# Strassen products for the FFN input of a two-layer diffusion trunk, and a new place for layer 1's tables

## The chip, the cores and the metric

The kernel runs on one core of a Trainium2 chip. The time is device microseconds (us) of one execution. Five engines take part: TensorE (PE, matmuls; PEld is its weight load), VectorE (DVE), ScalarE (ACT), GpSimd (POOL), and SyncE (SP), which issues most of the DMAs. Each engine runs its own instructions in order, and semaphores tie the engines together.

## The reference, cut to what matters

The program computes one step of a trunk of two layers over 640 tokens (512 latent, 128 context) of width 1024. Each layer mixes the tokens by four branches (a state-space model, a Fourier transform, attention, a short convolution), merges them by gates, projects, and then runs an FFN:

```
x  = x + g_m * mix
xn = rms_norm(x, lp['norm_ffn_g']) * (1 + sc_f) + sh_f
x  = x + g_f * swiglu(xn, lp['w_ffn_in'], lp['w_ffn_out'])
```

Here `swiglu` is `(silu(xn @ Wg) * (xn @ Wu)) @ Wo`, `Wg` and `Wu` being the halves of `w_ffn_in`. The FFN width is 2816, that is 22 tiles of 128 channels. Shift, scale and gate (`sh_f`, `sc_f`, `g_f` and the same for the mixer) are six sections of a modulation, `silu(cond) @ w_ada + b_ada`, for each layer and stream. Everything is float32.

## The kernel before, in words

**Layout.** All activations are channel-major: a tile holds 128 channels by 640 tokens, in two halves of 320 (`HALF`), each half in a PSUM bank of its own. A float32 product is made of three: an operand `x` is split into a rounded `xh` and a rest `xl`, a weight into `whi` and `wlo`, and the sum is `whi*xh + wlo*xh + whi*xl`. So one chunk (128 output channels, 1024 input channels) is 8 k-tiles x 3 terms x 2 halves = 48 matmuls of 128x128 by 320 columns, all issued at line 238 (`mm`). In the trace `main` is the PSUM tile of a chunk (two banks, two such tiles), `side` that of the smaller products.

**Weights** (`weights`, L317 on). A chunk's weights are loaded by SP to `wraw`, ACT casts them to `whi` (L319), DVE subtracts to get `wlo` (L320). There are three tiles each of `wraw`, `whi`, `wlo` (`WBUFS`). Around a norm, four chunks are subtracted by POOL instead of DVE (`SPARE`, L332 and L333).

**Order.** PE's order is written by hand: a main stream of products, and side chains (generators) whose steps are put between them at `tick()` when an estimated clock says that they are ready. On the other engines a scheduler orders the work, where the weights run up to 400 instructions ahead (`AHEAD`). [...]

**Stages of a layer.** `mixer_in` (input projection; latents, attention, convolution), `mixer_out` (state-space blocks, gates, merges), `tail` (output projection, norm, FFN). In the first layer the state-space tables of that layer (`ssm_tables`) are made beside `mixer_in`, the modulations' sections 2 to 5 beside `mixer_out`. The tables and rotations of layer 1 and all six modulation sections of layer 1 are made beside `tail` of layer 0. A modulation step on DVE is `ada_j` at L572.

**The FFN** (`tail`, L1488 on). `normed` makes the eight operand tiles `xs[k] = (xh, xl)` from the norm: a DVE multiplication to a scratch tile `hh` or `hl` (L458), an ACT bias and rounding to `xh` (L461), and a DVE operation for `xl` (L463). The first pair of chunks runs beside it. Then, for f = 0 to 21, `ffn_in(f)` makes a gate chunk and an up chunk, ACT takes the silu (L1521), DVE multiplies (`f_s`, L1523), and the product is split to `hh` and `hl`. `FFN_ROUNDS` are (0,8), (8,16), (16,22): after a round's tiles are there, eight output chunks of `wfo` run over them and are added to `x` (L1332, `residual`). One tile of the next round is made ahead of the output chunks. In the last round the last three output chunks go by halves of the tokens, and then the next layer's norm, or the output, follows.

The core of the FFN's input before:

```
def ffn_in(f):
    pg = self.chunk(A["wfi"][l, f], KD, xs) if f else first[0]
    s = self.t(p, [128, NT], "f_s", bufs=2)
    nc.scalar.activation(out=two(s), in_=pg[:, :, :HALF], func=AF.Silu)
    pu = self.chunk(A["wfi"][l, NF + f], KD, xs) if f else first[1]
    self.anchor = nc.vector.tensor_mul(out=two(s), in0=pu[:, :, :HALF], in1=two(s))
    self.split(hi, lo, s)
    hs[f] = (hi, lo)
```

## Time and profile before

| | us |
|---|---|
| median of 3 runs (2669.23 to 2675.43) | 2671.71 |
| span of the profiled execution | 2683.6 |
| PE busy | 2618.7 (98%), 18518 instructions |
| DVE busy | 1534.2 (57%) |
| ACT busy | 883.2 (33%) |
| POOL busy | 187.9 (7%) |

The profiled execution is 11.9 us (0.45%) longer than the median of the timed runs. The busy shares are means over stages that differ; the windows in the section of rows give them stage by stage. Their bounds are read off the instructions: a layer's first latent copy and its last attention DMA bound the first window (59.5 to 422.5, and 1401.1 to 1755.2), from there to the first residual is the second (to 832.0 and to 2148.6), and the first to the last `f_s` product of the FFN is the third (910.1 to 1331.8 and 2229.6 to 2637.9). PEclk in a row is the granted clock as a share of the full 2.4 GHz.

### The profile page before, as it was taken

To read this page: it belongs to the slowest core of one execution; us is meant where nothing else is said; L and a number is where in the kernel's file an instruction comes from. 1 tells how busy PE (TensorE), PEld (TensorE's weight loads), DVE (VectorE), ACT (ScalarE), POOL (GpSimd) and SP (SyncE) were. 2 spreads that over 40 slices of the span, in tenths; PEclk is the share of its full clock that TensorE was granted. 3 is DMA by queue.
4 is the path that set the end of the run, shared out by engine and by line. 5 is a ranking of instruction groups with operands and counts; after the bars stand their busy time and mean duration, and the time that the engine had idled before them with its cause. 6 is when DMAs were issued, how large, how long until landed. Compare 5 with 4: busy or idle time off the path is not lost.

```text
span 2683.6 us, 44723 instructions
## 1 busy us (share of the span) xinstructions
PE 2618.7 (98%) x18518; PEld 2505.7 (93%) x18518; DVE 1534.2 (57%) x3061; ACT 883.2 (33%) x1393; POOL 187.9 (7%) x316
## 2 busy tenths in 40 slices
PE   7999999999999999999999899999999999999999
PEld 5987898999999899999979779999999999999999
DVE  5888764776557579989453356654454444232323
ACT  5334544233224422221243244433323233212211
POOL 0110000111001100000020000011100010000000
PEclk8999999999999999999999999999999999999999
DMA  6442115574435255655232221155532322222222
GB/s 250 135 150 85 56 61 173 176 216 140 126 121 172 63 165 181 202 179 166 80 119 75 60 63 52 50 155 160 149 99 80 107 74 71 79 72 79 71 75 75
DMA packets 118747, 312.78 MB, mean 117 GB/s; under 512 B 35344, under 2 KB 46160, under 8 KB 118288
## 3 DMA queue, kind: packets, MB, share of 16 engines
q1 hardware_dynamic: 99376, 250.52, 30.7%
q0 software_dynamic: 16432, 55.39, 6.1%
q10 hardware_dynamic: 2736, 4.01, 0.4%
q8 instruction: 146, 2.39, 0.4%
q14 instruction: 57, 0.47, 0.1%
HBM read 267.07 MB, written 42.80 MB: 115 GB/s over the span
## 4 chain that ended last, share of the span: by engine, by line
PE 84%; issue 9%; DVE 2%; ACT 2%; DMA 2%; POOL 0%; ACTq 0%; SPq 0%; DVEq 0%; POOLq 0%
PE main L238 74%; PE side L238 9%; PE side L242 1%; DMA s_EF<-d_et 1%; DVE xl L463 1%; DVE wlo L320 0%; ACT whi L319 0%; ACT pq L897 0%; DVE hl L458 0%; ACT P L794 0%; DMA yb<-d_br 0%; POOL d_r L1136 0%; DVE hh L458 0%; DVE sm L791 0%; ACT xh L461 0%
## 5 line engine op out<-in xcount | busy, mean ns | idle before, releaser
L238 PE MATMUL main<-xh,whi 128*128 128x320 f32 x3488 | 831.2, 315 | 1.7 <-ACT xh L461 1.3
L238 PE MATMUL main<-xl,whi 128*128 128x320 f32 x3488 | 815.8, 311 | 1.7 <-DVE xl L463 1.5
L238 PE MATMUL main<-xh,wlo 128*128 128x320 f32 x3488 | 813.5, 310 | 0.0
L319 ACT CAST whi<-wraw 128x1024 fp32r<-128x1024 f32 (+1 forms) x302 | 312.3, 1034 | 1162.4 <-PE main L238 675.9
L238 PEld LDWEIGHTS main<-xh,whi 128*128 128x128 f32 x3488 | 585.7, 189 | 25.1 <-issue 19.9
L238 PEld LDWEIGHTS main<-xl,whi 128*128 128x128 f32 x3488 | 590.4, 189 | 6.7 <-DVE xl L463 6.4
L320 DVE TENSOR_TENSOR wlo<-wraw,whi 128x1024 fp32r<-128x1024 f32 (+1 forms) x302 | 367.7, 1218 | 397.0 <-ACT whi L319 395.7
L238 PEld LDWEIGHTS main<-xh,wlo 128*128 128x128 f32 x3488 | 590.5, 189 | 0.0
L238 PE MATMUL main<-yb,whi 128*128 128x320 f32 x1152 | 231.3, 312 | 2.1 <-ACT yb L319 2.1
L572 DVE SCALAR_TENSOR_TENSOR ada_j<-ada,ada_c 128x1024 bf16<-128x1024 f32 x160 | 195.1, 1219 | 3.8 <-DMA ada<-wada 2.9
L238 PEld LDWEIGHTS main<-yb,whi 128*128 128x128 f32 x1152 | 184.7, 189 | 3.0 <-ACT yb L319 2.4
L1332 DVE SCALAR_TENSOR_TENSOR x<-main,ada,x 128x320 f32<-128x320 f32 (+2 forms) x192 | 75.6, 434 | 177.2 <-PE main L238 176.9
L238 PE MATMUL main<-hh,whi 128*128 128x320 f32 x704 | 167.4, 311 | 0.0
L238 PE MATMUL main<-hh,wlo 128*128 128x320 f32 x704 | 166.2, 309 | 0.0
L238 PE MATMUL main<-hl,whi 128*128 128x320 f32 x704 | 166.2, 309 | 0.0
L238 PE MATMUL main<-yb,wlo 128*128 128x320 f32 x576 | 131.9, 310 | 0.0
L1523 DVE TENSOR_TENSOR f_s<-main,f_s 128x640 f32<-128x640 f32 x44 | 36.2, 824 | 150.6 <-PE main L238 150.6
L238 PEld LDWEIGHTS main<-hh,whi 128*128 128x128 f32 x704 | 119.0, 188 | 3.5 <-issue 3.5
L238 PEld LDWEIGHTS main<-hh,wlo 128*128 128x128 f32 x704 | 119.2, 188 | 0.0
L238 PEld LDWEIGHTS main<-hl,whi 128*128 128x128 f32 x704 | 119.2, 188 | 0.0
L238 PEld LDWEIGHTS main<-yb,wlo 128*128 128x128 f32 x576 | 97.1, 189 | 0.0
L794 ACT ACTIVATE P<-side,sm,rq 128x640 f32<-128x640 f32 (+1 forms) x80 | 63.9, 800 | 98.7 <-DVE sm L792 97.0
(320 smaller groups left out, 2761.3 us busy)
## 6 DMA issues: line engine op xcount, KB each, us to landing
ada<-wada SPq DMA_DIRECT2D x96, 512.0 KB, 4.4
wraw<-wfi SPq DMA_DIRECT2D x88, 512.0 KB, 3.6
wraw<-wgate SPq DMA_DIRECT2D x64, 512.0 KB, 3.6
wraw<-win SPq DMA_DIRECT2D x50, 512.0 KB, 3.7
wraw<-wbr SPq DMA_DIRECT2D x32, 512.0 KB, 3.7
wraw<-wfo SPq DMA_DIRECT2D x32, 512.0 KB, 3.6
d_f<-t_G POOLq DMA_DIRECT2D x16, 512.0 KB, 4.1
d_et<-t_et POOLq DMA_DIRECT2D x16, 512.0 KB, 5.1
```

Of the source, the lines that this page charges most:

```text
L238: self.nc.tensor.matmul(out, lhsT, rhs, **kw)
L242: self.nc.tensor.transpose(out, in_, ident)
L319: self.nc.scalar.copy(out=hi, in_=src)
L320: self.nc.vector.tensor_sub(out=lo, in0=src, in1=hi.bitcast(F32))
L463: nc.vector.scalar_tensor_tensor(out=xl[:, a:b], in0=t[:, a:b], scalar=B[:, s:s + 1], in1=xh.bitcast(F32)[:, a:b], op0=ALU.add, op1=ALU.su ...
L572: nc.vector.scalar_tensor_tensor(out=junk, in0=w, scalar=1.0, in1=sc[:, s, :], op0=ALU.mult, op1=ALU.mult, accum_out=self.ada[l][:, o + t, ...
L794: nc.scalar.activation(out=p[:, :nk].rearrange("p (a b) -> p a b", a=s.shape[1]), in_=s, func=AF.Exp, scale=rq, bias=small[:, 1:2], accum_ ...
L1332: self.anchor = nc.vector.scalar_tensor_tensor(out=x[:, o:o + n], in0=p, scalar=gcol[:, s:s + 1], in1=x[:, o:o + n], op0=ALU.mult, op1=ALU ...
L1523: self.anchor = nc.vector.tensor_mul(out=two(s), in0=pu[:, :, :HALF], in1=two(s))
```

## The change

Five things are altered; comments are taken out of the file too, so its line numbers differ.

1. **Seven half products.** For f = 2 to 21 (`PLAIN = 2`) the pair of a gate and an up chunk is seen as a 2x2 block product, the blocks being the two halves of the input channels (4 k-tiles each) by the two halves of the tokens on one side, and the gate and up weights by the same halves on the other. Seven products of 4 k-tiles and 320 columns take the place of eight. `strassen_weights` adds four sums of weight halves (128x512 each) to the two loaded chunks, `sums` makes the four sums of operand tiles (T1 to T4) after f = 0, and `place` writes T1 over the second half of `xs[0..3]`.
2. **PSUM.** In `tail` the main tiles are four of one bank each (`main_bank`), where there were two of two banks.
3. **Rounds.** `FFN_ROUNDS` is (0,6), (6,12), (12,18), (18,22), and `hh` and `hl` have 7 tiles in place of 9, to make room.
4. **Tables.** Layer 1's `ssm_tables` and `rotations` move from `tail` of layer 0 to `mixer_in` of layer 1, where layer 0's stand too.
5. **Modulations.** Beside `tail` of layer 0 stand sections 0 and 1 of layer 1 alone; sections 2 to 5 move to `mixer_out` of layer 1.

```
-FFN_ROUNDS = [(0, 8), (8, 16), (16, 22)]
+FFN_ROUNDS = [(0, 6), (6, 12), (12, 18), (18, 22)]
+PLAIN = 2
-TABLES_PACE = (1.5, 3.0)
+TABLES_PACE = 1.5
-MOD_PACE = (10.5, 7.0)
+MOD_PACE = (10.5, 12.0)
...
+    def strassen_weights(self, first, second, ahead=AHEAD):
...
+            a, b = raw
+            pair([a[:, :n]])
+            sa, sb = [self.t(self.sp, [128, 1024], "wsum", bufs=2) for _ in range(2)]
+            V.tensor_add(out=sa[:, :m], in0=b[:, :m], in1=b[:, m:n])
+            V.tensor_add(out=sa[:, m:n], in0=sa[:, :m], in1=a[:, :m])
+            pair([sa[:, :n]])
+            V.tensor_add(out=sb[:, :m], in0=sa[:, m:n], in1=a[:, m:n])
+            pair([sb[:, :m], b[:, m:n]])
+            V.tensor_add(out=sb[:, m:n], in0=a[:, :m], in1=b[:, :m])
+            pair([sb[:, m:n]])
+        return out
+
+    def strassen(self, first, second, forms, use):
+        ws = self.strassen_weights(first, second)
+        a, b, c, d = [self.main_bank()[:, :HALF] for _ in range(4)]
+        self.bank = (self.bank + 1) % 4
+        n = first.shape[1] // 2
+        for i, (bank, x, step, start) in enumerate((
+                (a, "B11", "P1", True), (b, "B21", "P2", True), (c, "T1", "P5", True), (a, "T2", "U2", False),
+                (c, "B22", "P3", False), (d, "T4", "P4", True), (a, "T3", "U3", False))):
+            hi, lo, o = ws[i]
+            for k in range(n):
+                xh, xl = forms[x][k]
+                for t, (ww, xx) in enumerate(((hi, xh), (lo, xh), (hi, xl))):
+                    self.mm(bank, ww[:, o + 128 * k:o + 128 * k + 128], xx, start=start and k == 0 and t == 0,
+                            stop=k == n - 1 and t == 2, skip_group_check=not start)
+                self.tick()
+            use(step, bank)
...
+    def sums(self, pool, tags, bs, B, xs):
...
+        for k in range(KD):
+            for a, b, s in ((0, LAT, 0), (LAT, NT, 1)):
+                nc.scalar.activation(out=bs[k][:, a:b], in_=bs[k][:, a:b], func=AF.Identity, bias=B[:, k, s:s + 1])
...
+            V.tensor_sub(out=t1, in0=b11, in1=b12)
+            V.scalar_tensor_tensor(out=t24[:, :HALF], in0=t1, scalar=-1.0, in1=b22, op0=ALU.mult, op1=ALU.subtract)
+            V.tensor_sub(out=t3[:, o], in0=b22, in1=b12)
+            V.tensor_add(out=t24[:, HALF:], in0=t24[:, :HALF], in1=b21)
+            todo = [(t24, ("T2", "T4"))] + ([(t3, ("T3", "T3"))] if k % 2 else [])
+            for t, names in todo:
+                hi, lo = [self.t(pool, [128, NT], tag, F32R, bufs=6) for tag in ("th", "tl")]
+                self.split(hi, lo, t)
...
+        def place():
+            for k in range(n):
+                hi, lo = forms["T1"][k]
+                self.split(hi, lo, t1s[k // 2][:, k % 2 * HALF:k % 2 * HALF + HALF])
...
+            def halves(f):
...
+                def use(step, ps):
+                    if step in ("P1", "U2", "P5"):
+                        nc.scalar.copy(out={"P1": s0, "U2": s1, "P5": u1}[step], in_=ps)
+                    elif step == "P4":
+                        nc.scalar.activation(out=u0, in_=ps, func=AF.Copy, scale=-1.0)
+                    elif step == "U3":
+                        self.anchor = V.tensor_tensor(out=two(u), in0=ps.unsqueeze(1).to_broadcast([128, 2, HALF]),
+                                                      in1=two(u), op=ALU.add)
+                    else:
+                        o = s0 if step == "P2" else s1
+                        V.tensor_add(out=o, in0=ps, in1=o)
+                        nc.scalar.activation(out=o, in_=o, func=AF.Silu)
+                self.strassen(A["wfi"][l, f], A["wfi"][l, NF + f], forms, use)
+                V.scalar_tensor_tensor(out=s, in0=u, scalar=-1.0, in1=s, op0=ALU.mult, op1=ALU.mult)
+                split_h(f, s)
...
-                hi = self.t(p, [128, NT], "hh", F32R, bufs=9)
-                lo = self.t(p, [128, NT], "hl", F32R, bufs=9)
+                hi = self.t(p, [128, NT], "hh", F32R, bufs=7)
+                lo = self.t(p, [128, NT], "hl", F32R, bufs=7)
...
-                self.tables = self.side(self.layer_tables(pt, l + 1, TABLES_PACE[1]))
-                self.modulations(pt, l + 1, range(6), MOD_START[1], MOD_PACE[1], 2)
+                self.modulations(pt, l + 1, range(2), MOD_START[1], MOD_PACE[1], 1)
...
-            if l == 0:
-                self.modulations(p, 0, range(2, 6), MOD_START[0], MOD_PACE[0], 1)
+            self.modulations(p, l, range(2, 6), MOD_START[0], MOD_PACE[0], 1)
```

In all, PE's order has 480 matmuls fewer than before, DVE's 521 instructions more and ACT's 401 more.

On DVE, inside the FFN of layer 1 away from its ends, one pair of chunks before is two weight subtractions, the product `f_s` and its rest `hl`:

```order
L320 TENSOR_TENSOR wlo_23972<-wraw_23969,whi_23971 128x1024 [waits DMAHW4_49,Activation_49]
L1523 TENSOR_TENSOR f_s_23850<-main_23858,f_s_23850 128x640 [waits PE_49,Activation_49]
L320 TENSOR_TENSOR wlo_24032<-wraw_24029,whi_24031 128x1024 [waits DMAHW5_49,Activation_49]
L320 TENSOR_TENSOR hl_23909<-f_s_23850,hh_23908 128x640 [waits Activation_49]
L320 TENSOR_TENSOR wlo_24089<-wraw_24086,whi_24088 128x1024 [waits DMAHW6_49,Activation_49]
```

The same pair now, from the addition of P2 (L1656) on; L1652 is the addition of U3, L1659 the last product, `wsum` the weights' sums, and the four groups of `wlo` are called A1 (22907), A2 (22915), A3 (22920, in two) and A4 (22927):

```order
L1656 TENSOR_TENSOR f_s_22768<-main_3283_22799,f_s_22768 128x320 [waits PE_49]
L321 TENSOR_TENSOR wlo_22907<-wraw_22902,whi_22906 128x1024 [waits Activation_49]
L1656 TENSOR_TENSOR f_s_22768<-main_3284_22800,f_s_22768 128x320 [waits PE_49,Activation_49]
L321 TENSOR_TENSOR wlo_22915<-wsum_22910,whi_22914 128x1024 [waits Activation_49]
L1652 TENSOR_TENSOR f_u_22769<-main_3282_22798,f_u_22769 128x640 [waits PE_49,Activation_49]
L321 TENSOR_TENSOR wlo_22920<-wsum_22911,whi_22919 128x512 [waits DVE_49,Activation_49]
L321 TENSOR_TENSOR wlo_22920<-wraw_22903,whi_22919 128x512 [waits Activation_49]
L389 TENSOR_TENSOR wsum_23042<-wraw_23035 128x512 [waits DMAHW3_49,DVE_49]
L1659 SCALAR_TENSOR_TENSOR f_s_22768<-f_u_22769,f_s_22768 128x640 [waits DVE_49]
L390 TENSOR_TENSOR wsum_23042<-wsum_23042,wraw_23034 128x512 [waits DMAHW2_49,DVE_49]
L321 TENSOR_TENSOR wlo_22927<-wsum_22911,whi_22926 128x512 [waits Activation_49]
L321 TENSOR_TENSOR hl_22897<-f_s_22768,hh_22896 128x640 [waits Activation_49]
```

Where four instructions stood for a pair there are 14 now (the two sums that begin the next group of weights follow the last row).

On DVE at the start of the same FFN, from the last operand of the norm to the first `f_s` products, before:

```order
L463 SCALAR_TENSOR_TENSOR xl_21718<-hl_21885,ada_87,xh_21717 128x128 [waits Activation_49]
L1523 TENSOR_TENSOR f_s_21920<-main_21732,f_s_21920 128x640 [waits PE_49,Activation_49]
L320 TENSOR_TENSOR wlo_22047<-wraw_22044,whi_22046 128x1024 [waits DMAHW3_49,Activation_49]
L320 TENSOR_TENSOR hl_21924<-f_s_21920,hh_21923 128x640 [waits Activation_49]
L320 TENSOR_TENSOR wlo_22104<-wraw_22101,whi_22103 128x1024 [waits DMAHW4_49,Activation_49]
```

Now, around the products of f = 1 (`f_s_22563`, by halves, L1681), with the first T1 tile at `xl_22224`, the other operand sums at L569 to L572 and their rests `tl`:

```order
L570 SCALAR_TENSOR_TENSOR hl_22494<-hh_22483,hl_22303 128x320 [waits DVE_49]
L321 TENSOR_TENSOR tl_22491<-hh_22485,th_22490 128x640 [waits Activation_49]
L572 TENSOR_TENSOR hl_22494<-hl_22494,hl_22303 128x320 [waits DVE_49]
L321 TENSOR_TENSOR wlo_22656<-wsum_22647,whi_22655 128x512 [waits Activation_49]
L321 TENSOR_TENSOR wlo_22656<-wraw_22639,whi_22655 128x512 [waits Activation_49]
L321 TENSOR_TENSOR tl_22500<-hl_22494,th_22499 128x640 [waits Activation_49]
L321 TENSOR_TENSOR tl_22504<-hl_22484,th_22503 128x640 [waits Activation_49]
L1681 TENSOR_TENSOR f_s_22563<-main_3244_22572,f_s_22563 128x320 [waits PE_49]
L1681 TENSOR_TENSOR f_s_22563<-main_3245_22573,f_s_22563 128x320 [waits PE_49]
L321 TENSOR_TENSOR wlo_22663<-wsum_22647,whi_22662 128x512 [waits Activation_49]
L321 TENSOR_TENSOR xl_22224<-hh_22459,xh_22223 128x320
```

The sums and their rests stand ahead of the products of f = 1, and the T1 tiles behind them.

On ACT at that place before, the two silus (L1521) have weight casts between them:

```order
L1521 ACTIVATE f_s_21920<-main_21731 128x640 [waits PE_49]
L332 CAST whi_21986<-wraw_21984 128x1024 [waits DMAHW2_49,Pool_49]
L319 CAST whi_22046<-wraw_22044 128x1024 [waits DMAHW3_49,PE_49,Pool_49]
L319 CAST hh_21923<-f_s_21920 128x640 [waits DVE_49]
L319 CAST whi_22103<-wraw_22101 128x1024 [waits DMAHW4_49,PE_49,Pool_49]
L1521 ACTIVATE f_s_21982<-main_21933 128x640
```

Now, from the first half of the silu of f = 1 (L1678) on; `th` are the rounded T2 to T4, `xh_22223` to `xh_22229` the rounded T1:

```order
L1678 ACTIVATE f_s_22563<-main_3238_22513 128x320 [waits PE_49]
L320 CAST whi_22650<-wsum_22646 128x1024 [waits PE_49,Pool_49]
L320 CAST th_22475<-hl_22470 128x640 [waits DVE_49]
L320 CAST th_22479<-hl_22460 128x640
L1678 ACTIVATE f_s_22563<-main_3239_22514 128x320
L320 CAST xh_22223<-hh_22459 128x320 [waits PE_49]
L320 CAST xh_22225<-hh_22459 128x320 [waits PE_49]
L320 CAST xh_22227<-hh_22483 128x320 [waits DVE_49,PE_49]
L320 CAST th_22490<-hh_22485 128x640 [waits DVE_49]
L320 CAST xh_22229<-hh_22483 128x320 [waits DVE_49,PE_49]
```

The rounding of T1, which waits for PE's last reading of the place that it overwrites, now stands ahead of the last three of the `th` casts.

## Rows read from the trace of the kernel before

**Rows 1.** The page: the span, and busy time by engine.
```profile
span 2683.6 us, 44723 instructions
PE 2618.7 (98%) x18518; PEld 2505.7 (93%) x18518; DVE 1534.2 (57%) x3061; ACT 883.2 (33%) x1393; POOL 187.9 (7%) x316
```

**Rows 2.** The chain that ended last: start us, us, engine and line, instructions.
```profile
2226.22 453.82 PE main L238 x3091
```

**Rows 3.** Six windows (layer 0, then layer 1): busy us and instructions.
```profile
core 0: us, PE busy (x) PEld busy (x) DVE busy (x) ACT busy (x) POOL busy (x), PEclk, DMA share, GB/s
59.50:422.50 363.00, 346.32 (x2694) 310.10 (x2695) 283.39 (x802) 158.17 (x290) 31.98 (x52) 0.98 0.32 101
422.50:832.00 409.50, 403.01 (x2771) 401.99 (x2771) 260.90 (x366) 131.34 (x195) 44.18 (x91) 0.98 0.54 166
910.10:1331.80 421.70, 421.70 (x3106) 418.50 (x3106) 330.56 (x704) 100.61 (x133) 25.46 (x37) 1.00 0.51 159
1401.10:1755.20 354.10, 333.54 (x2380) 301.85 (x2379) 173.94 (x394) 141.78 (x250) 10.15 (x15) 0.98 0.21 65
1755.20:2148.60 393.40, 392.64 (x2738) 392.08 (x2738) 187.41 (x221) 127.00 (x191) 41.29 (x88) 0.99 0.42 127
2229.60:2637.90 408.30, 408.30 (x2786) 408.30 (x2785) 122.05 (x149) 86.80 (x102) 2.41 (x1) 1.00 0.25 75
```

**Rows 4.** PE's timeline in the last chunks (start us, us, engine, operation).
```profile
2672.08 0.31 PE L238 MATMUL main<-hh,wlo 128*128 128x320 f32 x1
2672.23 0.31 PE L238 MATMUL main<-hl,whi 128*128 128x320 f32 x1
```

**Rows 5.** PE's timeline in the second stage of layer 0: two waits.
```profile
441.47 0.57 PE L238 MATMUL main<-yb,whi 128*128 128x320 f32 x2 [2.11 <-ACT yb L319]
...
610.38 1.96 PE L238 MATMUL side<-s_u,s_EF 128*128 128x80 f32 x8 [3.43 <-DMA s_EF<-d_et]
```

**Rows 6.** ACT's timeline ahead of the first of these waits: a step of the modulation.
```profile
435.20 1.91 ACT L560 ACTIVATE ada_c<-ada_c 128x2048 f32<-128x2048 f32 x1
```

**Rows 7.** A window around the second wait, the columns as in Rows 3.
```profile
605.00:620.00 15.00, 11.57 (x58) 11.33 (x57) 2.06 (x2) 6.82 (x18) 4.22 (x8) 0.66 0.34 80
```

**Rows 8.** DVE's timeline beside the norm of layer 1's FFN, and after it.
```profile
2201.63 0.54 DVE L458 SCALAR_TENSOR_TENSOR hl<-x,mod,side 128x320 f32<-128x320 f32 x1
2202.08 0.54 DVE L458 SCALAR_TENSOR_TENSOR hh<-x,mod,side 128x320 f32<-128x320 f32 x1
...
2210.89 2.45 DVE L463 SCALAR_TENSOR_TENSOR xl<-hh,ada,xh 128x320 fp32r<-128x320 f32 x1
```

**Rows 9.** DVE's groups by form: count | busy us, mean ns | idle before, releaser.
```profile
L320 DVE TENSOR_TENSOR wlo<-wraw,whi 128x1024 fp32r<-128x1024 f32 x278 | 344.7, 1240 | 380.4 <-ACT whi L319 379.5
L572 DVE SCALAR_TENSOR_TENSOR ada_j<-ada,ada_c 128x1024 bf16<-128x1024 f32 x160 | 195.1, 1219 | 3.8 <-DMA ada<-wada 2.9
...
L1523 DVE TENSOR_TENSOR f_s<-main,f_s 128x640 f32<-128x640 f32 x44 | 36.2, 824 | 150.6 <-PE main L238 150.6
L320 DVE TENSOR_TENSOR hl<-f_s,hh 128x640 fp32r<-128x640 f32 x44 | 36.0, 818 | 0.0
...
L998 DVE TENSOR_TENSOR t_tmp<-t_bb,t_pb 128x512 f32<-128x512 f32 x16 | 11.1, 691 | 0.4
```

**Rows 10.** ACT's groups by form, the same columns.
```profile
L319 ACT CAST whi<-wraw 128x1024 fp32r<-128x1024 f32 x278 | 292.3, 1051 | 1085.0 <-PE main L238 622.8 <-issue 452.0 <-DMA s_M<-d_k 7.2
L319 ACT CAST hh<-f_s 128x640 fp32r<-128x640 f32 x44 | 31.9, 725 | 4.6 <-DVE f_s L1523 4.4
...
L433 ACT ACTIVATE hl<-x 128x320 f32<-128x320 f32 x12 | 5.6, 470 | 15.5 <-DVE x L1332 15.5
```

**Rows 11.** POOL's timeline beside the last row of Rows 8.
```profile
2210.63 2.37 POOL L333 TENSOR_TENSOR wlo<-wraw,whi 128x1024 fp32r<-128x1024 f32 x1 [1.98 <-ACT whi L332]
```

**Rows 12.** The end of the program: PE's last matmul in its timeline.
```profile
2679.71 0.31 PE L238 MATMUL main<-hl,whi 128*128 128x320 f32 x1
```

**Rows 13.** The same place on DVE.
```profile
2680.06 0.68 DVE L1332 SCALAR_TENSOR_TENSOR x<-main,ada,x 128x192 f32<-128x192 f32 x2 [1.96 <-PE main L238]
```

More of the change, by code (lines that the diff above doesn't have):

```diff
@@ L336, in weights, with main_banks, main_bank @@
         return hi, lo
-    def main_ps(self):
-        return self.t(self.ps, [128, 2, 512], "main", bufs=2)
+    def main_banks(self, single):
+        if self.mp is not None:
+            self.mp.release()
+        self.single = single
+        self.mp = self.tc.alloc_tile_pool(name=self.nm("psm"), bufs=1, space=PSUM, reuse_waits="tile")
+    def main_bank(self):
+        self.bank = (self.bank + 1) % 4
+        return self.t(self.mp, [128, 512], f"main{self.bank}")
+    def main_ps(self):
+        if self.single:
+            return [self.main_bank() for _ in range(2)]
+        return self.t(self.mp, [128, 2, 512], "main", bufs=2)
@@ L597, in low_rank @@
                 f = tile()
-                nc.scalar.copy(out=f.rearrange("p (a b) -> p a b", a=2), in_=ps[:, :, :HALF])
                 q = tile()
-                nc.scalar.activation(out=q.rearrange("p (a b) -> p a b", a=2), in_=ps[:, :, :HALF], func=AF.Square)
+                for b, fv, qv in self.pieces(ps, f, q):
+                    nc.scalar.copy(out=fv, in_=b)
+                    nc.scalar.activation(out=qv, in_=b, func=AF.Square)
                 raw.append(f)
@@ L1531, in tail @@
                 if r == len(FFN_ROUNDS) - 1 and not last:
-                    self.need(self.tables)
                     self.need(self.modside)
@@ L1581, in emit @@
                         self.tap(f"xh{l}_{k}", xs[k][0].bitcast(F32))
-                self.mixer_in(l, xs, first, tables if l == 0 else None)
+                if l > 0:
+                    tables = tc.alloc_tile_pool(name=f"p0t{l}", bufs=2, side="right", reuse_waits="tile")
+                self.mixer_in(l, xs, first, tables)
                 ms = self.mixer_out(l, xs)
```

124 lines of the change are left out of this document (95 added, 29 removed).

## The prediction

> **What bounds the kernel now.** I read the page first, for which engine is full, then the chain that ended last, for what sets the end, then windows by stage, then single rows for durations. PE is busy 98% of a span of 2683.6 us, DVE 57%, ACT 33% [rows 1]. The chain is PE's products nearly throughout: its longest piece is 453.82 us of 3091 matmuls without a release from another engine [rows 2]. So a matmul of 320 columns costs 453.82 / 3091 = 0.1468 us, and what the kernel loses is what it computes, plus the few places where PE stands. In both FFN windows PE is busy in every microsecond, and its granted clock is 1.00, that is 2.4 GHz [rows 3]. A matmul taken from there is worth its full 0.1468 us, provided that nothing waits in its place. The price holds where one bank takes product after product as well: 2672.08 to 2672.23 is the same step [rows 4], so a change of weights for each matmul, which the seven half products need, has no price of its own.
>
> **The sum** is made against the profiled span and carried as a difference to the median, 2671.7; the span is 11.9 us (0.45%) longer than it.
>
> **1. Products: -70.5.** A pair of chunks is 96 matmuls, and is now 7 x 4 x 3 = 84. With 20 pairs in each of two layers, 480 go, as PE's order shows. 480 x 0.1468 = 70.5.
>
> **2. Layer 1's tables: -4.5.** They leave the FFN window of layer 0, which is 421.7 long against 408.3 in layer 1, where nothing stands beside it, both full: -13.4. They go where layer 0's stand, beside the input stage. That stage takes 363.0 with tables and 354.1 without [rows 3]: +8.9. PE is not full in either, so part of the tables fills holes there. SP gets one small load more, and POOL the tables' own transfers, in a stage where layer 0's POOL carries the same.
>
> **3. Modulations of layer 1 in its second stage: +13.** Layer 0's second stage, with them, is 409.5, layer 1's without is 393.4 [rows 3]: 16.1 is the upper bound. From below: two waits there of 2.11 and 3.43 us [rows 5]. Ahead of the first stands a modulation step of 1.91 us on ACT [rows 6], behind which the cast of `yb` comes. After the second the clock falls to 0.66 on average over 15 us [rows 7]: PE at half its rate for some 10 us loses 5.1 us, and the shorter wait costs less. Waits and clock give about 10. I take 13, between the two; zero stays possible, as these waits also hang on transfers that arrive at other times in layer 1. SP's loads for the modulations stand between the weights' there; layer 0's stage has them too, at a DMA share of 0.54 [rows 3], so the difference holds them.
>
> **4. The step from plain pairs to half products: +27.4.** This is new, and the trace shows only its pieces. The unit prices: DVE's operations overlap slightly. A 320-column operation lasts 0.54 us, and the next starts 0.45 to 0.46 us after it (2201.63, 2202.08) [rows 8], 0.09 less than its length. Taking 0.09 off each form [rows 9]: 1024 columns 1.15, 640 columns 0.74, 512 columns 0.60. On ACT [rows 10], likewise, 1024 columns 0.95, 640 columns 0.63, 320 columns 0.37.
> First, four weight sums now stand on DVE ahead of operands of the norm, on which the first pair waits: 4 x 0.60 = 2.4, and about 1.0 for the sixteen bias operations on ACT among them: 3.4 a layer.
> Second, during f = 1 PE has 96 x 0.1468 = 14.1 us of products. DVE has in the same time sixteen sums (7.4), six rests of 640 (4.4), three groups of `wlo` (3.5), an `hl` and two weight sums (1.9): 17.2; then f = 0's product (0.9, and a handover of 0.2) and a held operation: where POOL subtracts weights for 2.37 us [rows 11], a 320-column operation on DVE took 2.45 instead of 0.54 [rows 8], about 2 more. That is 20.3 us. Behind it, in DVE's order, stand f = 1's own product (0.9), a `wlo` of 512 (0.6), the first T1 rest (0.46), two weight sums, an `hl` and three more T1 rests (3.3): 25.6. P1 and P2 need none of this; P5, the third product, would end at 14.1 + 3 x 12 x 0.1468 = 19.4. With its fourth T1 tile at 25.6, a handover and its last three matmuls it ends at 26.3. PE stands 6.9 us. ACT adds to it rather than hides it: the T1 casts there wait for PE's last reading of f = 1, and two `th` casts queue behind them, for which DVE's next rests wait.
> Third, after a stall of such length the clock falls. After the 3.43 us wait 5.1 us were lost [rows 7]; after the shorter one in [rows 5] less; I take 3.4.
> Together 13.7 a layer, 27.4 for both. The bounds for one layer: 4, if P1, P2 and slack of the scheduler take nearly all of the backlog, and 20, if each of the three is at its upper end (5, 10, 5).
>
> **5. The last round: +2.4.** It has four tiles instead of six. The last `hh` and `hl` are needed 18 x 0.147 = 2.64 us after the last pair's end for the second chunk to go on (before, it was 30 x 0.147 = 4.4). The chain from U3 is addition 0.82, product 0.88, `hh` 0.73 [rows 10], `hl` 0.82 [rows 9], and handovers; a handover from PE is 0.35 us from the last matmul's start to DVE's (2679.71 and 2680.06) [rows 12, 13]. That is 3.8: 1.2 a layer, 0 to 3.
>
> **6. Half products in a row: +2.** For one pair PE has 84 x 0.1468 = 12.33 us. DVE has by its spacing two `wlo` of 1024 (2.3), three of 512 (1.8), four sums of 512 (2.4), two additions of 320 (0.92), an addition, a product and an `hl` of 640 (2.2): 9.65. It is not free to run ahead: in its order the second `wlo` (A2) stands behind P3's addition, and ACT's cast of A2 behind the silu of that addition, so DVE stands there for 0.37 + 0.95 and the handovers, some 1.6. The loop is 11.2, under 12.33: nothing. ACT has 6.3 in a pair. Beside it the modulations of sections 0 and 1 still put about 11 times two steps of 1.15 us in such pairs in layer 0; they fit in the two holes (before A1 and before A2), or nearly: +2. A fourth round adds eight more residual groups and weight chunks a layer, about 8.5 us of DVE, beside output products where DVE is free more than half the time: 0.
>
> **Sum:** -70.5 - 4.5 + 13 + 27.4 + 2.4 + 2 = -30.2. 2671.7 - 30.2 = 2641.5, given as 2642.
>
> **Rivals.**
> *The step is hidden and the modulations are nearly free*: 4 a layer and +4. -70.5 - 4.5 + 4 + 8 + 1 = -62: 2610. For it speaks that the norm's operands ran beside PE before with holes on DVE [rows 8]; against it that DVE's backlog as counted is longer than f = 1's products.
> *The step costs its upper bound*, 20 a layer, and the modulations 16: -70.5 - 4.5 + 16 + 40 + 5 = -14: 2658.
> *DVE's operations don't overlap in the pair's chain.* Most of them read what ACT or DVE has just written, where those of [rows 8] are independent. At their full durations [rows 9] they are 10.9, the loop is 12.6 with ACT's share, 0.3 longer than PE's; with the modulations in, 14.0, 1.7 longer in some 11 pairs. 40 x 0.3 + 11 x 1.7 = 31, of which about 1.5 a layer goes into the slack that the first pairs have: +28 on the forecast, 2670, no change. The Trainium skill ("VectorE: DVE Perf Modes", section "The DRAIN you can't avoid") says that after each operation the next one doesn't start until the pipe is empty, unless nothing holds it. The rows of this trace show starts 0.09 us before the end, so by them it doesn't bind.
> *PE waits at every handover* (the slower side). Before, a chunk had two banks and the next chunk another two; now a bank is taken again within a pair: P3 adds onto P5's bank, U2 and U3 onto P1's, each after ACT has copied it. The copy has one product of slack, 12 x 0.1468 = 1.76 us. A copy of 0.47 [rows 10] and handover of 0.35 make 0.8, so it holds unless ACT is at a 1024-column cast (1.05) when PE ends, where 0.8 + 1.05 = 1.85 passes it, and two in a row pass it by 1.1. If PE stood 1 us in each pair and the clock lost 1.7 behind it, that is 2.7 x 40 = 108: 2750. The kernel is slower than before from 30.2 / 40 = 0.76 us a pair on. Against it: ACT is busy a third of the time, and its casts wait for free buffers, that is mostly for the ends of other products. The Trainium skill ("TensorE: Matmul & The Clock Gate", section "A second HAM failure mode: psum-queue depth-cycling") tells of a kernel whose cycling through banks with small waits let the clock swing between its levels. The rows here, cycling between two double tiles, show 1.00 in both FFN windows; four single banks no row shows.
> That the change doesn't do what it says is left out: PE's order has the 480 fewer.
>
> **How the numbers follow.** Forecast 2642: 0.50. Hidden step, 2610: 0.14. Dear step, 2658: 0.11. No overlap, 2670: 0.13. Handovers, 2750: 0.12. The range leaves out the handovers and part of the hidden step's lower side: 2612 to 2670. A measurement of this kernel can tell some 0.2% (5.3 us) from no change. Faster by more: 0.50 + 0.14 + 0.11, and 0.05 of the no-overlap case: 0.80. Within: 0.08. Slower: 0.12.
>
> **What would show it.** Right: in both FFNs, 84 matmuls in 12.33 us a pair at clock 1.00; one stall of 5 to 9 us ahead of the first P5 in each layer, released by DVE's `xl` (the first T1 tiles), with the clock at half behind it; an FFN window in layer 1 of about 408.3 - 35.3 + 11.5 = 384.5, and in layer 0 little more; the input stage of layer 1 near 363, its second stage near 406. Wrong: DVE or ACT as releaser of PE inside the steady pairs (then it is one of the last two rivals, DVE's `wlo` for the one, ACT's copies for the other); no stall at P5 (then 2610); a longer start of layer 1, if the tables come late for the stage that reads them.

## The result, and the profile after

The changed kernel takes 2627.02 us (median of 4 runs, 2626.33 to 2628.97); the kernel before took 2671.19 beside it. The ratio is 0.9826, with a 95% interval of 0.9811 to 0.9841: 44 us, or 1.7%, faster. Forecast were 2642 and a difference of 30 us, with a range of 2612 to 2670.

The profiled execution of after is 2624.6 us long, close to its median. That of before was 12 us over its own ([rows 1] and the table above), and this matters below.

The page of after, span and busy time by engine, which answers to [rows 1]:

```profile
span 2624.6 us, 44979 instructions
PE 2550.9 (97%) x18038; PEld 2437.4 (93%) x18038; DVE 1802.2 (69%) x3581; ACT 1054.2 (40%) x1793; POOL 188.9 (7%) x316
```

PE has 480 instructions fewer. DVE has taken 268 us more and still isn't the bound.

From here on the stages of a layer are cut at the same three instructions in every kernel: the first latent copy, the last attention transfer and the first residual (the place where DVE first waits for one). "Input", "second stage" and "tail" are the stretches between them, and the tail reaches to the next layer's first latent copy, or to the end. The windows of after (length, busy us and instructions of PE, PEld, DVE, ACT, POOL, then granted clock, DMA share, GB/s), layer 0's three stages and then layer 1's:

```profile
58.90:420.30 361.40, 344.66 (x2695) 309.81 (x2696) 283.36 (x803) 158.21 (x290) 31.93 (x53) 0.99 0.32 100
420.30:820.30 400.00, 396.61 (x2754) 395.25 (x2753) 259.02 (x354) 130.93 (x194) 42.66 (x88) 0.99 0.53 168
820.30:1355.00 534.70, 522.30 (x3469) 503.90 (x3468) 372.96 (x641) 233.41 (x403) 24.30 (x21) 0.99 0.32 98
1355.00:1718.40 363.40, 346.13 (x2713) 311.48 (x2713) 285.34 (x828) 164.21 (x305) 35.01 (x54) 0.99 0.31 101
1718.40:2116.70 398.30, 395.58 (x2755) 394.99 (x2755) 258.98 (x354) 131.00 (x194) 42.58 (x88) 0.99 0.54 168
2116.70:2624.60 507.90, 497.79 (x3334) 489.20 (x3332) 315.42 (x523) 206.77 (x356) 10.12 (x5) 0.99 0.26 78
```

In the first, second, fourth and fifth row the stages are those of [rows 3]. The input stage of layer 1 went from 354.1 to 363.4 (forecast: near 363), its second stage from 393.4 to 398.3 (forecast: near 406). But layer 0's second stage, in which nothing was changed, went from 409.5 to 400.0.

The steady half products wait for nothing. All that PE waits for on other engines from 2195 us to 2620 us of after, that is in the whole FFN of layer 1, is this (engine, tile and line, releaser: us in total, times, longest):

```profile
PE main L239 <- DVE xl L321: 2.3, 2, 1.5
PE main L239 <- DVE f_s L1681: 1.3, 1, 1.3
PE main L239 <- ACT hh L320: 0.5, 1, 0.5
```

The first two lines are the one place that the prediction named, the first T1 product; the third is the `hh` of the last round. PE's timeline at the first T1 product, and DVE's rests of the four T1 tiles (L321) that release it:

```profile
2215.32 0.31 PE L239 MATMUL main<-xl,whi 128*128 128x320 f32 x1
2216.92 0.39 PE L239 MATMUL main<-xh,whi 128*128 128x320 f32 x1 [1.29 <-DVE f_s L1681]
2217.15 0.31 PE L239 MATMUL main<-xh,wlo 128*128 128x320 f32 x1
2218.23 0.41 PE L239 MATMUL main<-xl,whi 128*128 128x320 f32 x1 [0.77 <-DVE xl L321]
...
2220.57 0.63 PE L239 MATMUL main<-xl,whi 128*128 128x320 f32 x1 [1.48 <-DVE xl L321]
2221.00 0.47 PE L239 MATMUL main<-xh,whi 128*128 128x320 f32 x1
2221.27 0.47 PE L239 MATMUL main<-xh,wlo 128*128 128x320 f32 x1
...
2217.70 0.47 DVE L321 TENSOR_TENSOR xl<-hh,xh 128x320 fp32r<-128x320 f32 x1
...
2220.04 1.28 DVE L321 TENSOR_TENSOR xl<-hh,xh 128x320 fp32r<-128x320 f32 x3
```

P5 first waits for the bank, which the product of f = 1 (`f_s`) has to leave, and then for the rests of the T1 tiles, one by one. From start to start the three steps take 1.60, 1.08 and 1.95 us in place of 0.147: 4.2 us are lost. Behind it the steps are 0.27 instead of 0.147. Windows of 5 us around the start of the FFN and around this place show the clock:

```profile
2190.00:2195.00 5.00, 5.00 (x21) 5.00 (x21) 4.81 (x16) 5.00 (x15) 0.00 (x0) 0.53 0.01 3
2195.00:2200.00 5.00, 5.00 (x36) 5.00 (x35) 2.47 (x4) 4.78 (x10) 2.24 (x1) 1.00 0.00 0
...
2220.00:2225.00 5.00, 4.43 (x16) 4.43 (x17) 1.72 (x5) 0.80 (x2) 0.00 (x0) 0.50 0.00 0
```

At 2190 PE runs at half its clock too (21 matmuls where the next window has 36), after three shorter waits of 1.05, 0.39 and 0.52 us for the norm's operands, which stand behind the new weight sums and bias operations on DVE and ACT (busy 4.8 and 5.0 of 5 us).

### The profile page after: what moved, and what is told of

It reads as the page before. It is cut to its first block, busy times and chain, and to the rows that moved or that the text cites. A ratio compares the mean times of both kernels' runs of the same rounds, so it can differ in the third digit from the quotient of the medians.

```text
span 2624.6 us, 44979 instructions
## 1 busy us (share of the span) xinstructions
PE 2550.9 (97%) x18038; PEld 2437.4 (93%) x18038; DVE 1802.2 (69%) x3581; ACT 1054.2 (40%) x1793; POOL 188.9 (7%) x316
## 4 chain that ended last, share of the span: by engine, by line
PE 80%; issue 10%; DVE 5%; ACT 3%; DMA 2%; POOL 0%; SPq 0%; ACTq 0%; DVEq 0%; POOLq 0%
PE main L239 71%; PE side L239 8%; PE side L243 1%; DVE wlo L321 1%; DMA s_EF<-d_et 1%; DVE xl L543 1%; DMA s_M<-d_k 0%; ACT xh L541 0%; DVE sm L918 0%; ACT whi L320 0%; DVE tl L321 0%; ACT pq L1024 0%; DMA yb<-d_br 0%; DVE hh L569 0%; POOL d_r L1257 0%
## 5 line engine op out<-in xcount | busy, mean ns | idle before, releaser
L239 PE MATMUL main<-xh,wlo 128*128 128x320 f32 x2848 | 721.5, 311 | 0.0
L320 ACT CAST whi<-wraw 128x1024 fp32r<-128x1024 f32 (+2 forms) x318 | 297.5, 936 | 775.4 <-PE main L239 622.5
L239 PEld LDWEIGHTS main<-xh,whi 128*128 128x128 f32 x2848 | 493.8, 190 | 33.0 <-issue 20.0
L239 PEld LDWEIGHTS main<-xl,whi 128*128 128x128 f32 x2848 | 498.0, 189 | 11.9 <-DVE xl L321 5.9
L239 PEld LDWEIGHTS main<-xh,wlo 128*128 128x128 f32 x2848 | 498.7, 190 | 0.0
L321 DVE TENSOR_TENSOR wlo<-wraw,whi 128x1024 fp32r<-128x1024 f32 (+2 forms) x318 | 345.0, 1085 | 221.4 <-ACT whi L320 218.4
L696 DVE SCALAR_TENSOR_TENSOR ada_j<-ada,ada_c 128x1024 bf16<-128x1024 f32 x160 | 194.9, 1218 | 4.5 <-DMA ada<-wada 3.8
L239 PE MATMUL main<-th,whi 128*128 128x320 f32 x480 | 149.3, 311 | 0.0
L239 PE MATMUL main<-th,wlo 128*128 128x320 f32 x480 | 149.2, 311 | 0.0
L239 PE MATMUL main<-tl,whi 128*128 128x320 f32 x480 | 149.0, 310 | 0.0
L321 DVE TENSOR_TENSOR wlo<-wsum,whi 128x512 fp32r<-128x512 f32 (+1 forms) x120 | 103.7, 864 | 52.0 <-ACT whi L320 50.7
```

The costliest lines, as they stand in the source:

```text
L239: self.nc.tensor.matmul(out, lhsT, rhs, **kw)
L320: self.nc.scalar.copy(out=hi, in_=src)
L321: self.nc.vector.tensor_sub(out=lo, in0=src, in1=hi.bitcast(F32))
L696: nc.vector.scalar_tensor_tensor(out=junk, in0=w, scalar=1.0, in1=sc[:, s, :], op0=ALU.mult, op1=ALU.mult, accum_out=self.ada[l][:, o + t, ...
```

## The experiments

**The kernel before once more.** It was run unchanged for a second trace.

> The kernel before, unchanged, for a second trace of it: the profiled execution that the prediction was made from was 12 us over the median, and its second stage of layer 0 was 9.5 us longer than the same stage of the changed kernel, whose instructions there are the same. If that stage was only disturbed in that one execution, it takes about 400 us here and the span is about 2670; if it belongs to the kernel, it takes 409 again.

Its runs beside it took 2672.15 in the median, but single ones 2667.6 to 2682.4. The profiled one was long again: span 2678.9. Its second stages, layer 0 and layer 1:

```profile
421.80:828.40 406.60, 402.24 (x2770) 400.88 (x2769) 260.68 (x366) 131.27 (x195) 43.88 (x91) 0.98 0.53 167
...
1751.50:2144.00 392.50, 392.49 (x2738) 392.16 (x2738) 187.70 (x221) 126.86 (x191) 42.12 (x88) 0.99 0.41 127
```

So it is neither 400 nor 409. In the twelve other traces of this study (the changed kernel, and all experiments but this one) layer 0's second stage took 398.1 to 404.7. What differs is the landing of one transfer. The DMA issues between 590 and 600 us, here:

```profile
s_EF<-d_et SPq DMA_DIRECT2D x1, 1024.0 KB, 11.0
```

and in the next experiment, where it was issued at 597.0 us instead of 596.8:

```profile
s_EF<-d_et SPq DMA_DIRECT2D x1, 1024.0 KB, 6.4
```

In the trace that the prediction was made from it took 13.0 us. PE waited 3.43 us for it there and then ran at half clock [rows 5, 7], 1.5 us here, and not at all in the next. Over all fourteen traces it landed after 6.4 to 13.0 us, so the long wait belongs to single executions of the same instructions. Whether the modulations' loads make it likelier isn't shown: the stage without them was traced only twice. Why the landing scatters wasn't tried.

**The moves alone.** Parts 4 and 5 of the change were put on the kernel before.

```
-                self.tables = self.side(self.layer_tables(pt, l + 1, TABLES_PACE[1]))
-                self.modulations(pt, l + 1, range(6), MOD_START[1], MOD_PACE[1], 2)
+                self.modulations(pt, l + 1, range(2), MOD_START[1], MOD_PACE[1], 1)
...
+                if l > 0:
+                    self.tables = self.side(self.ssm_tables(tables, l, TABLES_PACE[0]))
...
+            self.modulations(p, l, range(2, 6), MOD_START[0], MOD_PACE[0], 1)
```

> The kernel before with parts 4 and 5 alone (layer 1's tables and rotations in its own input stage, sections 2 to 5 of its modulations in its own second stage). By the prediction's terms the tables bring -4.5 and the modulations cost 13: 2680, slower by 8.5. By the trace of after, where layer 1's second stage is only 4.8 us longer than before, the two cancel: 2671, within 3 us. If what they left behind in the FFN of layer 0 was hidden there, it is slower by 13 to 18: 2685 to 2690.

1.0004 of before, 0.9989 to 1.002: no difference (+1 us, -3 to +5). The windows say how that comes about: the tail of layer 0, then the three stages of layer 1:

```profile
821.40:1380.10 558.70, 555.21 (x3723) 539.04 (x3722) 254.48 (x458) 160.29 (x227) 26.16 (x24) 1.00 0.30 95
1380.10:1738.20 358.10, 340.34 (x2699) 306.40 (x2699) 265.62 (x750) 154.25 (x282) 32.97 (x51) 1.00 0.32 101
1738.20:2144.10 405.90, 401.82 (x2776) 401.18 (x2776) 259.83 (x355) 132.04 (x195) 43.08 (x89) 0.99 0.53 167
2144.10:2673.30 529.20, 524.67 (x3553) 516.55 (x3551) 176.54 (x261) 122.06 (x159) 9.58 (x4) 1.00 0.23 74
```

In before_again the same four are 569.1, 354.0, 392.5 and 534.9. Layer 0's tail gives 10.4, the input stage takes 4.1, and the last two, taken together since the first residual stands at another place among PE's products, take 7.7: +1.4 in all.

That place of the residual blurs the cut: DVE comes to it 4.5 us ahead of the residual itself in layer 1 of before, and 1.9 us ahead in after. PE's own products are a sharper cut, since every kernel has the same 2623 of them from a layer's first product of a `yb` tile (the branches' outputs) to its last. Layer 1's input stage from PE's last product of an `hl` tile in layer 0 to its first of a `yb` tile, for before, the moves alone and the next experiment; then the second stage, for layer 0 of before, and for layer 1 of before, the moves alone and after:

```profile
1381.08:1770.99 389.91, 367.82 (x2581) 332.85 (x2579) 194.58 (x442) 158.50 (x280) 18.82 (x32) 0.97 0.24 74
1358.60:1752.71 394.11, 374.89 (x2901) 337.67 (x2899) 284.78 (x796) 172.89 (x313) 41.58 (x68) 0.99 0.33 108
1357.52:1760.99 403.47, 384.66 (x2902) 344.69 (x2901) 286.78 (x801) 174.60 (x319) 41.77 (x68) 0.97 0.32 105
...
437.44:824.27 386.83, 380.34 (x2626) 379.32 (x2624) 251.94 (x344) 121.97 (x186) 37.21 (x73) 0.98 0.53 158
1770.99:2145.80 374.81, 374.05 (x2625) 373.49 (x2624) 181.25 (x214) 120.12 (x183) 35.80 (x73) 1.00 0.40 121
1752.71:2135.61 382.90, 378.82 (x2626) 378.18 (x2625) 251.85 (x344) 122.19 (x186) 37.12 (x73) 0.99 0.51 159
1733.00:2111.30 378.30, 375.58 (x2625) 374.99 (x2624) 251.74 (x344) 121.71 (x186) 37.15 (x73) 1.00 0.52 161
```

By these cuts layer 0's tail gives 14.2 (556.8 to 542.6), the input stage takes 4.2, the second stage 8 to 9 in this execution, and layer 1's tail nothing (537.8 and 537.7). In before_again the second stage takes 373.8. Of the twelve traces with modulations there, nine take 377.6 to 380.2, so 3 to 6 more; the other three take 382.9 to 383.3, and in each of these a transfer of `s_EF` landed after 10.9 us or more, as in the three longest stages of layer 0.

**No half products.** The changed kernel with `PLAIN` at 22 and without `sums`.

```
-PLAIN = 2
+PLAIN = NF
...
-                if f == 0:
+                if f == 0 and PLAIN < NF:
                     forms, place = self.sums(p, self.ntags, bs, self.ada[l][:, 24:32, :], xs)
```

> The changed kernel with PLAIN at 22: all pairs plain, no operand sums, the single banks, four rounds and the moves kept. 40 pairs take 1.76 us more each, 70.4. By the prediction's terms 27.4 us of the step to half products go: 2627 + 70.4 - 27.4 = 2670. By the trace of after, where the waits around that step are about 4.5 us in each FFN and the clock falls for a few us behind them, 13 to 16 go: 2681 to 2684. If the half products wait inside the pairs as well, it is below 2670.

1.0018 (1.0003 to 1.0033): 2677 by the ratio, 2679.2 the median. Against the moves alone the fourth round and the single banks cost some 4 us, with an uncertainty as large. By PE's products the two tails are only 0.9 and 0.4 longer than with the moves alone (543.5 and 538.1); the input stage of layer 1 is 9.4 longer (403.47 against 394.11 above), and 3.5 to 9.5 longer in the ten traces of the other kernels with a fourth round. Against after, the half products bring 51 us, not 70.4: the step to them costs some 19, within 6. Neither of the two times expected came: it lies between them.

**One plain pair more.**

```
-PLAIN = 2
+PLAIN = 3
```

> The changed kernel with one plain pair more (f = 2) ahead of the half products: 12 matmuls more in each layer, 3.5 us together, and 14 us more for VectorE's backlog. If the backlog of operand sums is what PE waits for at the first T1 product, the wait of 4.2 us and the clock behind it go in both layers: 2618 to 2621. If it is the order (T1 is written only when the last plain pair has read its place), the wait stands as before, one pair later: 2630.

0.9778 (0.9753 to 0.9802), 2616.5 in the median. It was timed again later, beside the changed kernel:

> plain3 a second time, beside the changed kernel: 2610 to 2617, so that the step's price in the changed kernel is 10 to 16 us over both layers, net of the 3.5 us of the two plain pairs.

> The changed kernel beside the next ones, on the same chip: 2625 to 2629, 0.982 to 0.984 of the kernel before.

2612.85 against 2625.70 there (0.9774 and 0.9821 of before). With 24 matmuls more it is 12.9 us faster than the changed kernel, within 6, and below both of the times that were expected. Its two tails:

```profile
816.00:1344.20 528.20, 520.89 (x3480) 502.98 (x3479) 368.67 (x631) 229.78 (x395) 24.29 (x21) 1.00 0.31 99
2104.90:2605.20 500.30, 494.83 (x3346) 486.25 (x3344) 310.88 (x514) 203.26 (x349) 10.10 (x5) 1.00 0.25 79
```

The tail of layer 1 is 32.4 us below that without half products, and 19 pairs x 1.76 are 33.4 (by PE's products the tails of both layers give 32.4). So after this one pair of breathing space the half products give nearly all that was counted for them, and the step, 507.9 - (500.3 - 1.8) = 9.4 us in layer 1, is gone. All that PE waits for in its FFN of layer 0 (900 to 1300 us):

```profile
PE main L239 <- ACT hh L320: 0.5, 1, 0.5
```

**Two plain pairs more** (`PLAIN = 4`).

> Two plain pairs ahead of the half products in place of one. If plain3 has nothing left of the step's price, two pairs more are plain and cost 2 x 1.76 = 3.5 us: 2615 to 2619. If some of it is left there, it is level with plain3 or below.

2621.05, 0.9804 (0.9786 to 0.9821), which is 8 us over plain3, with an uncertainty of some 6 for the difference, and over the range expected. Layer 1's tail is 502.0 against 500.3: the 1.7 us of one pair and nothing else. Part of the rest lies in the input stage of layer 1 (364.1 against 360.9 in plain3_again), which this edit doesn't touch.

**T1 first.** The step with its work in another order.

```
-            todo = [(t24, ("T2", "T4"))] + ([(t3, ("T3", "T3"))] if k % 2 else [])
+            todo = [(t24, ("T2", "T4"))]
+            if k % 2:
+                later.append(t3)
...
         def place():
-            for k in range(n):
-                hi, lo = forms["T1"][k]
-                self.split(hi, lo, t1s[k // 2][:, k % 2 * HALF:k % 2 * HALF + HALF])
+            with self.tc.high_priority(offset=40):
+                for k in range(n):
+                    hi, lo = forms["T1"][k]
+                    self.split(hi, lo, t1s[k // 2][:, k % 2 * HALF:k % 2 * HALF + HALF])
+            for t in later:
+                hi, lo = [self.t(pool, [128, NT], tag, F32R, bufs=6) for tag in ("th", "tl")]
+                self.split(hi, lo, t)
...
```

> The changed kernel (PLAIN = 2) with another order on VectorE at the step: the rests of the T1 tiles stand ahead of the products of f = 1, and the rounding and rests of the T3 tiles behind them, as U3 is the last of the seven to need them. No work is added or taken away. If PE's wait of 4.2 us at the first T1 product is the order in which the backlog is worked off, it falls below 1 us, and with the clock behind it each layer gains some 5: 2615 to 2618. If it is the backlog as a whole, the wait moves on to the T2 or T3 tiles: 2623 to 2628.

0.9795 (0.9778 to 0.9811), 2616.5: some 8 us below the changed kernel by the ratios, within 6, with as many instructions. Layer 1's tail is 502.5. What stays is PE's wait of 1.5 us for the bank that `f_s` leaves, and the waits at the start of the FFN (2.1 us for `xh`). Both were then taken up:

```
-                self.strassen(A["wfi"][l, f], A["wfi"][l, NF + f], forms, use)
+                self.strassen(A["wfi"][l, f], A["wfi"][l, NF + f], forms, use, 80 if f == PLAIN else AHEAD)
...
-                for b, sv in self.pieces(pu, s):
-                    self.anchor = nc.vector.tensor_mul(out=sv, in0=b, in1=sv)
+                with self.tc.high_priority(offset=60 if f == 1 else 0):
+                    for b, sv in self.pieces(pu, s):
+                        self.anchor = nc.vector.tensor_mul(out=sv, in0=b, in1=sv)
```

> t1_first (PLAIN = 2) with two things more in VectorE's order: the four weight sums of f = 2 stand behind the norm's operands rather than among them, and the product of f = 1 stands ahead of the last two T1 rests and of A3. The first takes the operands' delay at the start away (some 2 us and the clock behind it in each layer), the second the wait of 1.5 us for the bank that P5 takes. If these are what is left of the step, it is 2 x 2 us or so below t1_first and, with two plain pairs fewer, level with plain3 or up to 3 us below: 2608 to 2613. If VectorE's backlog only shifts the wait to U2 or P4: 2615 to 2620.

0.9777 (0.9756 to 0.9799), 2612.23, with a tail of 500.4 in layer 1: level with plain3, not better. The waits at the start fall to 0.7 us, so they came from the weight sums. The two pairs won are paid back by what stays of the step, in layer 1 a wait of 1.7 us for a T1 rest. This kernel, t1_first and plain3 are the fastest here; among them the runs don't decide.

**VectorE's room.** Additions that nothing reads were put into each pair of plain3, two in a first kernel and four, as here, in a second.

```
                 V.scalar_tensor_tensor(out=s, in0=u, scalar=-1.0, in1=s, op0=ALU.mult, op1=ALU.mult)
+                extra = self.t(p, [128, 512], "extra", bufs=1)
+                for _ in range(4):
+                    V.tensor_add(out=extra, in0=u[:, :512], in1=s[:, :512])
```

> plain3 with two additions of 128x512 more in VectorE's order behind the product of each pair of half products, which nothing reads: 1.2 us for each of 38 pairs. By the prediction's loop (11.2 of 12.33 us a pair) it just fits: within 3 us of plain3, 2612 to 2615. If VectorE's operations did not overlap, the loop would already be 12.6, and each pair would be longer by 1.2 to 1.4: 2660 or more.

> The same with four additions, 2.4 us a pair. By the prediction's loop, which has VectorE standing for ACT's cast in each pair, it is 13.6 of 12.33 us: 38 x 1.3 = 49, less the slack of the output rounds between the pairs: 2640 to 2660. If only VectorE's busy time counts (9.65 + 2.4 = 12.05), it is hidden: 2612 to 2616.

Two: 0.9792 (0.9773 to 0.9811), 4 us over plain3, which is within the uncertainty. Four: 0.982 (0.9806 to 0.9833), 2624.9, between the two times expected. But the two layers part. Layer 1's tail with four is 500.8, as before (500.3); layer 0's, where the modulations stand too, is 542.5 in place of 528.2. Two pairs of layer 1 with four additions each:

```profile
2244.00:2268.70 24.70, 24.70 (x170) 24.70 (x169) 24.04 (x38) 13.55 (x25) 0.00 (x0) 1.00 0.25 79
```

DVE is busy 24.04 us of 24.70 and PE doesn't wait. In plain3 a stretch of the same length (2230 to 2254.7) has it busy 18.59. In layer 0 PE waits for the late additions from PSUM, with two additions and with four:

```profile
PE main L239 <- DVE f_s L1656: 4.0, 2, 2.3
...
PE main L239 <- DVE f_s L1656: 8.7, 4, 3.2
```

So beside the modulations there is no room for two.

**A late copy in each pair.** The prediction's slower rival, built into plain3.

```
+                    if step == "P5":
+                        extra = self.t(p, [128, HALF], "extra", bufs=1)
+                        for _ in range(5):
+                            nc.scalar.copy(out=extra, in_=ps)
                     if step in ("P1", "U2", "P5"):
```

> plain3 with five more copies of P5's bank on ACT ahead of the one that is used, in each pair, so that P3, which takes the same bank again, must wait. This makes the prediction's slower rival on purpose, to price it. In ACT's order the used copy then stands behind the cast of the next A1, which waits for U2, so PE waits 1.5 to 2.3 us in each of 38 pairs: 57 to 87. If the clock falls behind each such wait, as the rival has it, some 1.7 more each, 65: 2735 to 2765. If it doesn't, 2670 to 2700.

1.0185 (1.0162 to 1.0207): 2719.9, between the two expectations, and 107 us over plain3. From 2240 us to the end PE waits in each of layer 1's 19 pairs, 2.0 us a time:

```profile
PE main L239 <- ACT f_u L1652: 38.2, 19, 2.2
```

One of them, on ACT and then on PE:

```profile
2400.31 2.26 ACT L1650 COPY extra<-main 128x320 f32<-128x320 f32 x5 [0.46 <-PE main L239]
2402.47 1.05 ACT L320 CAST whi<-wraw 128x1024 fp32r<-128x1024 f32 x1
2403.42 0.47 ACT L1661 ACTIVATE f_s<-f_s 128x320 f32<-128x320 f32 x1
2403.79 0.41 ACT L1652 COPY f_u<-main 128x320 f32<-128x320 f32 x1
```

```profile
2401.73 0.31 PE L239 MATMUL main<-tl,whi 128*128 128x320 f32 x1
2404.26 0.42 PE L239 MATMUL main<-xh,whi 128*128 128x320 f32 x1 [2.22 <-ACT f_u L1652]
```

The copy that releases the bank stands behind the five added ones (2.26 us), a cast of 1.05 us and a silu; the rival had the cast. Layer 1's tail grows by 560.4 - 500.3 = 60.1, 3.2 us a pair: from start to start PE loses 2.2 at the wait, and 1.0 to the clock in the mean. (This execution is 12 us over its median; by the median it is 2.8 a pair.) The clock stood at half for 3.4 to 3.7 us behind 11 of the 19 waits, not behind each; a window over one of those stretches:

```profile
2404.00:2409.00 5.00, 4.75 (x22) 4.75 (x23) 1.27 (x2) 1.00 (x3) 0.00 (x0) 0.66 0.33 105
```

## Why the prediction was right, and by how much it missed

The direction and the range held, and so did the reason: what leaves PE's full FFN windows is worth its time. The size was a third too small: 30 us forecast, 44 measured; the terms that add time were nearly all counted too high, above all the modulations and the step. Term by term:

| term | forecast | measured | from |
|---|---|---|---|
| 1 products | -70.5 | -68 to -70.4 | 480 x 0.1467; 1.7 a pair in plain4's tail; 32.4 for 19 pairs (33.4) in plain3's |
| 2 and 3, tables and modulations | +8.5 | +1 (-3 to +5) | the moves alone |
| 4 the step | +27.4 | +16 to +19 | plain3 beside after: 12.9 + 3.5, within 6; tails: 9.4 and 9.3 |
| 5 the last round (and the banks) | +2.4 | +4 (uncertain by as much) | no half products against the moves |
| 6 half products in a row | +2 | 0 | no wait in the pairs, both layers |
| sum | -30.2 | -44 to -49 | timed: -44 |

For the step in layer 0 the tails are those of both traces of each kernel, 535.0 - (527.5 - 1.8) = 9.3.

**1 and the bounding view** held. The price of 0.1468 us for a matmul from [rows 2], and that a single bank has no price of its own [rows 4], stand: 0.1467 in the steady half products of after.

**2 and 3 failed by one row.** The step that failed is the price of the modulations. Its upper bound of 16.1 was read as the difference of two windows of one execution [rows 3]. Some 4 of it are the cut: by PE's own products the two stages take 386.83 and 374.81, 12.0 apart. Some 8 are a transfer that landed late, and half a clock after it: in eleven of the fourteen traces the same products take 377.7 to 379.9. I took the same two waits [rows 5] as the lower bound, and called them waits that modulations bring; the longer hung on that transfer. What is left for the modulations is 3 to 6: the wait of 2.1 us for `yb`, which the traces without them in that stage don't have, and the clock behind it. The tables did better than forecast too: by PE's products 14.2 came out of the tail (forecast 13.4), and 4.2 went into the input stage (forecast 8.9). That the changed kernel's input stage took 363.4, as forecast, is in part luck: the moves alone take it to 358.1, and the rest comes with the rounds or the banks, for which the prediction had nothing there.

**4 was the right mechanism, mis-sized.** P5, released by DVE's T1 rests, with half a clock behind it, is what the trace shows, in both layers. The parts of 13.7 a layer were 3.4, 6.9 and 3.4; layer 1's 9.4 are 2.7 at the start (waits and half clock there lose 5.9, in plain3 3.2), 4.2 at P5, and 2.5 of half clock behind it. The 4.2 is a little under the stall of 5 to 9 that was named as a sign. The 6.9 is too much because DVE's backlog was shorter than counted: its fourth T1 rest ends at 2221.3, which is 23.4 us after the first product of f = 1 (2197.87) and not 25.6. I took 0.46 us for each 320-column operation from [rows 8]; those of the sums start every 0.40 (2202.31, 2202.72 and 2203.12 us for L570, L571 and L572), which is 1.1 us over sums and T1 rests. The operation that POOL holds came, 1.97 us beside a subtraction of 2.41 in place of 0.48, but took 0.6 less than counted, and half of f = 0's product ran ahead of f = 1 (0.4). The other 0.5 is PE's: it works at half clock while the last two rests come. The wait needs both the backlog and T1's place at its end: plain3 takes it away by time, t1_first by the order. That the order alone would do was not in the prediction.

**5** held in the tails only. PE waits 0.5 us for the last `hh` in each layer, where 1.2 was counted, and the tails without half products are 0.9 and 0.4 longer than with the moves alone. The input stage of layer 1, which follows the last round, is longer by 3.5 to 9.5; the prediction didn't have that, and what of it the rounds and what the banks cause wasn't separated.

**6 was right for a wrong reason.** DVE's loop of 11.2 us counted ACT's cast as time in which DVE stands in every pair. Four additions fit into 3 us of room without any effect in layer 1, so the standing is room, not part of the loop. (Probably ACT's casts are done by the time that a late DVE comes; that wasn't looked at.) Busy time by spacing, 9.3 us a pair in plain3, is what counts there. That +2 became nothing holds for the changed kernel; two additions in layer 0, beside the modulations, already make PE wait 4.0 us.

**The rivals.** *No overlap on DVE* is out: a loop of 12.6 would not have taken 2.4 us more for nothing. The trace adds where it does hold. An operation that reads what the one ahead of it wrote starts after its end, as these two weight sums in after do:

```profile
2319.75 0.69 DVE L389 TENSOR_TENSOR wsum<-wraw 128x512 f32<-128x512 f32 x1
2320.48 0.69 DVE L390 TENSOR_TENSOR wsum<-wsum,wraw 128x512 f32<-128x512 f32 x1
```

From start to start they take 0.73 us, where 0.60 is usual with another tile between. The Trainium skill ("VectorE: DVE Perf Modes", section "The DRAIN you can't avoid") says that a next operation which isn't held starts earlier. By that exception, not by the rule ahead of it, the trace agrees: with another tile between, the 0.69 us operations start 0.09 us before the end of the one ahead. *Handovers* didn't come, since PE waits for ACT nowhere inside a pair; late_copy shows a price of 3.2 a pair for waits of 2.0 us, where the rival's rule, the wait and 1.7 of clock, would give 3.7; what waits of 1 us cost no run shows. *The hidden step* (2610) didn't come with the changed kernel; plain3 comes to nearly its time, at 2613. Of *the dear step* nothing came.

One of the signs was wrong by itself: the FFN window of layer 1 (first to last `f_s`) was to be 384.5 and is 398.2 (2195.1 to 2593.3). The third and fourth rounds were cut differently, so two tiles of the last output chunks, 8 x 2 x 6 x 0.1468 = 14.1 us, now lie inside it instead of behind it: from the last `f_s` to the end after takes 31.3 us, before 45.7. That this is nearly the whole difference is chance, as of the 11.5 counted for the step only some 7 came. The sum didn't rest on it.

## What to carry to other kernels

A difference of two stages in one trace can hold an accident: before it becomes a price, look for a transfer that landed late in the longer one, and compare the stage with a second execution. Cut stages at instructions of the engine that bounds them; another engine's can stand at another place among them, which was 4 of 16 us here. Where a change of method needs prepared operands, the cost is in the first use. Let one piece of the old method run between, or prepare the operands in the order of their use: either got back 8 to 13 us here (each within 6), at no or almost no extra work. For an engine off the critical path count its busy time against the period; its waits for others in the loop were room here as long as it didn't fall behind. Count it with everything that runs beside it: layer 0 had less room than layer 1.

## What the runs showed of the hardware

The same transfer of 1 MB, issued at the same place of the program, landed after 6.4 to 13.0 us in fourteen executions; where one of its kind took 10.9 or more, PE's stage was 4 us or more longer than usual. Single runs of the kernel before lay between 2667 and 2682 us, and such waits with the clock behind them can be a part of that: both of its traced executions, 2678.9 and 2683.6 us long, held one. The clock fell to half behind single waits of about 2.0 us, but behind only 11 of 19, and at the start of after's FFN behind three of 1.05, 0.39 and 0.52 us in a row.
